# Two 64-row score products per head pair in two banks, and a two-pass first product of the compression, in a hybrid decoder block

## The chip, the cores and the metric

The kernel runs on one core of a Trainium2 chip. The metric is the device time of one execution in microseconds (us), as the median of several runs. Matrix products run on TensorE (PE in the rows, its weight loads PEld), elementwise work on VectorE (DVE) and ScalarE (ACT); GpSimd (POOL) and SyncE (SP) mainly issue transfers (DMA).

## The reference, cut to what matters

256 tokens of width 1024 go through one block. Two attention branches of 8 heads of 64 run side by side (with 256 tokens every block that a query may look at is selected, so branch A is causal attention and branch B is the gated sum of a compressed, a selected and a window part). A gated merge, an output projection and a mixture of 16384 one-neuron experts follow.

```python
# branch A, per head:  s = q k^T * scale ; causal mask ; softmax ; o = p v
s_own = jnp.einsum('hqd,hld->hql', qc, k_own)
# branch B, compressed keys and values, per group g:
blocks = t[:, idx] + pos_emb[None, None, :, None, :]
flat = blocks.transpose(0, 3, 1, 2, 4).reshape(B, G, n_cmp, CMP_LEN * D)
return jax.nn.gelu(flat @ w1 + b1) @ w2 + b2        # n_cmp = 15, CMP_LEN * D = 2048, w1: 2048 x 256
# branch B: o = g0 * o_cmp + g1 * o_slc + g2 * o_win, each a masked softmax over its keys
```

## The kernel before, in words

Float32 products whose result needs the accuracy are made from two rounded halves: a helper `split` (L104) lets ScalarE cast to a high half (`whi`, `hhi`, `bhi`) and VectorE subtract it to get a low half (`wlo`, `hlo`, `blo`). Each product is then three passes, high by high, high by low and low by high (`mm3`, L126). Weights come through `load_piece` (L109): a transfer of 512 KB into `wraw`, then a split, three buffers each.

**The order of the first stage.** PE runs the projections of the input (`token_proj`, `ps_proj`, L168 to L171), and among them the two calls of `compress` (L300): keys (kv = 0) after the second 512-wide projection, values (kv = 1) after the third. Then come four merge gates (`merge_gate` L378, products L121, L122 and L124 inside `cols_proj`, 24 products of 256 columns each). The queries and keys are normalised per head, rotated and transposed by `to_dt` (L256) into `qTA`, `qTB`, `kTA` and `kTB`, with the 64 dimensions of the two heads of a pair on the 128 partitions.

**The compression** (`compress`). The 30 blocks (2 groups of 15) have 2048 inputs each, 16 chunks of 128. Its first product `ph` (L129 to L131) has the 30 blocks as the stationary operand and 256 columns of `w1` as the moving one: 16 chunks by three passes, 48 products of 256 columns, in four weight pieces. Then `hrow` copies the result, two transposes `pht` (L323) turn it round, ScalarE applies the bias and the GELU (`hid`), and `po` (L330) is the second product.

**The attention** (`attn_unit`, L405). There are 24 units: for each half h of the 256 queries four pairs of heads of branch A, and four pairs by two kinds of branch B. With h = 0 a query sees 128 keys, with h = 1 it sees 256. A unit makes on PE a mask product (`ps_s`, L408, bfloat16, identity by mask, 256 columns), a score product (L410, float32), transposes of the probabilities (`ps_pt`, L427) and the output products (`ps_y`, `ps_yb`, L432, 64 columns of the array each). In between VectorE takes the maximum (L413), ScalarE two exponentials (L417), VectorE scales (L423), and ScalarE copies the transposes (L429). So that one score product gives both heads of a pair side by side, the keys are padded with zeros: `kTA` and `kTB` have the shape [128, 4, 2, 256], where slice j holds head j's keys in its own 64 partitions and zeros in the other 64. GpSimd writes the zeros at the start (L182, L183), and `to_dt` fills the keys with two half-height copies on ScalarE (L265). Before the first half of branch B ends, `ps_sc` (L449), `ps_pct` (L468) and `ps_yb` (L473) do the compressed part.

**PSUM.** In this stage eight banks are shared out as four tags of two: `s` (scores), `tp` (transposes), `y` (outputs) and `mg` (merge gates 4 to 15, and later the up and output projections). The instructions of one engine run in a fixed order, which a list scheduler sets when the program is built, from priorities, buffers and its own estimates; so it also puts products of gates 4 and 5 among the attention where it expects PE to wait.

Behind that come gates 4 to 15, the up projection (`ps_up`), the output projection (`ps_o`), the query projection of the experts (`ps_q`) and the two long expert stages (`ps_u` L588, `acc` L855).

## Time and profile before

| | us |
|---|---|
| median of 3 runs | 940.72 (939.09 to 942.44) |
| the profiled execution, its own time | 938.46 |
| its span | 936.7 |
| the stretch that the change touches, first product to last attention product | 0 to 159.4 |

The profile is read by stages: for each stretch the busy time of every engine, then, in the stretch that the change touches, the instructions in order of time. A row's start is exact to about 0.01 us; a PE row's own length contains the time until the result has left the array and overlaps the next row, so what a product costs PE is read from start to start. "[0.81 <-ACT hid]" at a row's end is idle time of the engine before it and what ended it.

### The profile page before, as it was taken

To read this page: it belongs to the slowest core of one execution; us is meant where nothing else is said; L and a number is where in the kernel's file an instruction comes from. 1 tells how busy PE (TensorE), PEld (TensorE's weight loads), DVE (VectorE), ACT (ScalarE), POOL (GpSimd) and SP (SyncE) were. 2 spreads that over 40 slices of the span, in tenths; PEclk is the share of its full clock that TensorE was granted. 3 is DMA by queue.
4 is the path that set the end of the run, shared out by engine and by line. 5 is a ranking of instruction groups with operands and counts; after the bars stand their busy time and mean duration, and the time that the engine had idled before them with its cause. 6 is when DMAs were issued, how large, how long until landed. Compare 5 with 4: busy or idle time off the path is not lost.

```text
span 936.7 us, 17034 instructions
## 1 busy us (share of the span) xinstructions
PE 900.6 (96%) x6433; PEld 842.9 (90%) x6433; DVE 614.3 (66%) x1663; ACT 309.6 (33%) x768; POOL 218.4 (23%) x213
## 2 busy tenths in 40 slices
PE   8999999999999999999999999999989989998987
PEld 6778867998899999999999999999988888988986
DVE  5886876577567689997778788644445544444444
ACT  6766776545541221326555455300000000000000
POOL 2000000000100223233232233333344333443330
PEclk9999999999999999999999999999999999999999
DMA  7665401556556999999999999999999999999994
GB/s 242 191 213 190 159 1 47 183 185 210 169 173 235 331 392 365 376 373 328 350 334 352 354 339 347 354 378 403 357 369 399 400 380 403 385 392 401 400 398 185
DMA packets 79570, 281.96 MB, mean 301 GB/s; under 512 B 10176, under 2 KB 10432, under 8 KB 79488
## 3 DMA queue, kind: packets, MB, share of 16 engines
q1 hardware_dynamic: 51088, 177.63, 52.6%
q0 software_dynamic: 28400, 103.25, 29.2%
q8 instruction: 51, 0.84, 0.3%
q14 instruction: 31, 0.25, 0.1%
HBM read 278.64 MB, written 1.05 MB: 299 GB/s over the span
## 4 chain that ended last, share of the span: by engine, by line
PE 56%; DMA 28%; issue 7%; POOL 3%; DVE 3%; ACT 2%; DVEq 0%; POOLq 0%; ACTq 0%; SPq 0%
PE ps_u L588 28%; DMA grow<-in_v_dram,gidx 21%; PE ps_g L819 4%; POOL grow L611 3%; DMA grow<-in_u_dram,gidx 3%; PE ps_q L121 2%; PE ps_mg L124 2%; PE ps_mg L121 2%; PE ps_q L124 2%; PE ps_q L122 2%; PE ps_mg L122 2%; PE ps_s L410 2%; PE ps_proj L171 1%; PE ps_pt L427 1%; DVE wlo L106 1%
## 5 line engine op out<-in xcount | busy, mean ns | idle before, releaser
L855 PE MATMUL acc<-ga,uvraw 128*128 128x160 f32 x2048 | 292.9, 302 | 21.3 <-DMA uvraw<-in_v_dram 19.5
L855 PEld LDWEIGHTS acc<-ga,uvraw 128*128 128x128 f32 x2048 | 279.9, 190 | 34.2 <-DMA uvraw<-in_v_dram 32.3
L588 PE MATMUL ps_u<-h2f,uvraw 128*128 128x160 f32 x2048 | 287.3, 299 | 0.0
L588 PEld LDWEIGHTS ps_u<-h2f,uvraw 128*128 128x128 f32 x2048 | 280.7, 190 | 0.1
L633 DVE SCALAR_TENSOR_TENSOR accG<-grow,gwt,accG 128x1024 f32<-128x1024 f32 x94 | 120.8, 1285 | 137.0 <-DMA grow<-in_v_dram,gidx 136.9
L611 POOL DMA_INDIRECT grow<-in_u_dram,gidx x96 | 102.1, 1063 | 302.2 <-DVE gdot L622 149.1
L611 POOL DMA_INDIRECT grow<-in_v_dram,gidx x96 | 106.0, 1104 | 166.0 <-DVE mark L857 150.0
L622 DVE CUSTOM_DVE_ANT_0 grow<-grow,h2d 128x1024 f32<-128x1024 f32 x96 | 116.7, 1218 | 34.6 <-DMA grow<-in_u_dram,gidx 34.5
L106 DVE TENSOR_TENSOR wlo<-wraw,whi 128x1024 fp32r<-128x1024 f32 (+1 forms) x80 | 95.5, 1196 | 37.1 <-ACT whi L105 37.0
L105 ACT CAST whi<-wraw 128x1024 fp32r<-128x1024 f32 (+1 forms) x80 | 82.0, 1029 | 65.5 <-PE ps_q L122 13.9
L868 ACT COPY accT<-acc 128x320 f32<-128x320 f32 x2 | 0.9, 426 | 270.9 <-PE acc L855 270.9
L592 ACT ACTIVATE ga<-ps_u 128x160 f32<-128x160 f32 (+32 forms) x124 | 33.5, 271 | 143.7 <-PE ps_u L588 143.4
L814 ACT ACTIVATE og<-o,gT 128x128 f16<-128x128 f16 x160 | 61.9, 568 | 15.9 <-PE ps_g L819 14.5
L819 PE MATMUL ps_g<-og,o 128*128 128x128 f16 x320 | 44.4, 294 | 0.0
L819 PEld LDWEIGHTS <-o 128*128 128x128 f16 x320 | 36.3, 116 | 1.5
L168 PE MATMUL ps_proj<-whi,hhi 128*128 128x512 f32 (+1 forms) x96 | 36.3, 381 | 1.3 <-ACT hhi L205 1.0
L489 POOL DMA_DIRECT2D gain<-in_g_dram x1 | 0.5, 533 | 151.2 <-DVE wlo L106 151.2
L169 PE MATMUL ps_proj<-whi,hlo 128*128 128x512 f32 (+1 forms) x96 | 35.7, 378 | 0.0
L121 PE MATMUL ps_mg<-hhi,whi 128*128 128x256 f32 x128 | 32.3, 288 | 0.0
L596 DVE TENSOR_TENSOR ga<-ga,au 128x160 f32<-128x160 f32 (+32 forms) x68 | 16.8, 247 | 23.4 <-ACT au L595 22.9
L122 PE MATMUL ps_mg<-hlo,whi 128*128 128x256 f32 x128 | 31.9, 285 | 0.0
L121 PE MATMUL ps_q<-h2hi,whi 128*128 128x256 f32 x128 | 31.7, 285 | 0.2 <-ACT h2hi L105 0.2
(256 smaller groups left out, 1126.0 us busy)
## 6 DMA issues: line engine op xcount, KB each, us to landing
uvraw<-in_uT_dram SPq DMA_DIRECT2D x128, 512.0 KB, 6.8
uvraw<-in_v_dram SPq DMA_DIRECT2D x128, 512.0 KB, 7.2
wraw<-in_wqkv_dram SPq DMA_DIRECT2D x20, 512.0 KB, 4.7
wraw<-in_wmg_dram SPq DMA_DIRECT2D x16, 512.0 KB, 3.6
wraw<-in_wq_dram SPq DMA_DIRECT2D x16, 512.0 KB, 4.3
wraw<-in_w1kv_dram SPq DMA_DIRECT2D x8, 512.0 KB, 4.0
wraw<-in_wup_dram SPq DMA_DIRECT2D x8, 512.0 KB, 3.6
wraw<-in_wout_dram SPq DMA_DIRECT2D x8, 512.0 KB, 4.5
```

The costliest lines, as they stand in the source:

```text
L105: nc.scalar.copy(hi, src)
L106: state["dve"] = nc.vector.tensor_sub(lo, src, hi)
L121: nc.tensor.matmul(ps, lh, rh, start=i == 0, stop=False)
L122: nc.tensor.matmul(ps, ll if lo_last else lh, rh if lo_last else rl, start=False, stop=False)
L124: nc.tensor.matmul(ps, lh if lo_last else ll, rl if lo_last else rh, start=False, stop=i == NC - 1)
L588: state["pe"] = nc.tensor.matmul(ps, raw[:, c * P:(c + 1) * P], h2f[:, c, NG:], start=c == 0, stop=c == NC - 1)
L611: nc.gpsimd.indirect_dma_start(out=dst, out_offset=None, in_=src, in_offset=bass.IndirectOffsetOnAxis(ap=gidx[:, j:j + 1], axis=0))
L622: nc.vector.tensor_tensor_reduce(out=g, in0=g, in1=h2d[k], scale=1.0, scalar=0.0, op0=ALU.mult, op1=ALU.add, accum_out=gdot[:, j:j + 1])
L633: nc.vector.scalar_tensor_tensor(accG[:, k], g, gwt[:, j:j + 1], accG[:, k], op0=ALU.mult, op1=ALU.add)
L814: nc.scalar.activation(og[0][:, :, k], o1[:, :, k], AF.Copy, scale=gT[:, t0 + k:t0 + k + 1])
L819: nc.tensor.matmul(ps[:, k, :], o2[:, :, k], og[i][:, :, k], start=i == 0, stop=i == 1, skip_group_check=True)
L855: nc.tensor.matmul(acc[c // 2][:, c % 2, 0:ND], raw[:, c * P:(c + 1) * P], ga_at(i), start=i == 0 and c % 2 == 0, stop=i == NKEY - 1, skip ...
```

## The change

- `attn_unit`: the score tile gets one bank per head (`bank2`, two banks, two buffers, tag `s2`). The mask product becomes two of 128 columns, and the score product becomes two products of 64 rows, one per head and bank, each with 128 (h = 0) or 256 (h = 1) columns.
- No zero padding: `kTB` is half as large, of `kTA` one slice is used, the four large fills on GpSimd go, and `to_dt` always makes one copy of full height.
- The tag `mg` is gone, since `s2` takes four banks: gates 4 to 15, `ps_sc`, `ps_up`, `ps_o` and a warming product now take one bank of an `s2` buffer.
- `compress`: the high and the low half of the blocks lie side by side as 60 stationary columns, so one pass of the high weights serves both; the low weights need a second pass with 30 columns. The two halves of the result are added by a product with two stacked identities (`twice`, fetched by two small transfers), in place of the transpose.

```diff
+    def bank2(name):
+        return psum[-1].tile([P, 2, 512], F32, name=name, tag="s2")
...
-        kTB = ap.tile([P, 4, 2, S], F32, name="kTB")
+        kTB = ap.tile([P, 4, S], F32, name="kTB")
...
-        for t in (kTA, kTB, kcT):
-            nc.gpsimd.memset(t[0:HD, :, 1], 0.0)
-            nc.gpsimd.memset(t[HD:P, :, 0], 0.0)
+        nc.gpsimd.memset(kcT[0:HD, :, 1], 0.0)
+        nc.gpsimd.memset(kcT[HD:P, :, 0], 0.0)
...
-            if len(dst.shape) == 3:
-                nc.scalar.copy(dst[:, :, h * P:(h + 1) * P], pt)
-            else:
-                for j in range(2):
-                    r = slice(j * HD, (j + 1) * HD)
-                    nc.scalar.copy(dst[r, :, j, h * P:(h + 1) * P], pt[r])
+            nc.scalar.copy(dst[:, :, h * P:(h + 1) * P], pt)
...
+        twice = ap.tile([P, 2 * N_CMP], F32, name="twice")
+        for i in range(2):
+            r = slice(2 * N_CMP * i, 2 * N_CMP * (i + 1))
+            nc.gpsimd.dma_start(twice[r], consts[r, r])
...
-            bhi = sp.tile([P, 16, 2 * N_CMP], F32R, name="bhi")
-            blo = sp.tile([P, 16, 2 * N_CMP], F32R, name="blo")
-            split(bhi, blo, blk.rearrange("p c g n -> p c (g n)"))
-            ph = bank("ph", "s")[0:2 * N_CMP, 0:256]
-            pairs = []
+            nb = 2 * N_CMP
+            bhl = sp.tile([P, 16, 2 * nb], F32R, name="bhl")
+            split(bhl[:, :, 0:nb], bhl[:, :, nb:], blk.rearrange("p c g n -> p c (g n)"))
+            ph = bank("ph", "s")[0:2 * nb, 0:256]
             for i in range(4):
                 hi, lo = load_piece(w1kv[kv][:, i * DM:(i + 1) * DM])
-                pairs += [((bhi[:, 4 * i + k], blo[:, 4 * i + k]),
-                           (hi[:, k * 256:(k + 1) * 256], lo[:, k * 256:(k + 1) * 256])) for k in range(4)]
-            mm3(ph, pairs)
+                for k in range(4):
+                    r, last = slice(k * 256, (k + 1) * 256), i == 3 and k == 3
+                    if last:
+                        nc.tensor.matmul(ph[0:nb], bhl[:, 4 * i + k, 0:nb], lo[:, r], start=False, stop=False)
+                    nc.tensor.matmul(ph, bhl[:, 4 * i + k], hi[:, r], start=i + k == 0, stop=last)
+                    if not last:
+                        nc.tensor.matmul(ph[0:nb], bhl[:, 4 * i + k, 0:nb], lo[:, r], start=False, stop=False)
...
-                nc.tensor.transpose(pht[:, hc, 0:2 * N_CMP], hrow[0:2 * N_CMP, hc], C("ident")[0:2 * N_CMP, 0:2 * N_CMP])
+                nc.tensor.matmul(pht[:, hc, 0:nb], hrow[0:2 * nb, hc], twice[0:2 * nb], start=True, stop=True,
+                                 skip_group_check=True)
...
-            ps = bank("ps_mg", tag)[:, :S]
+            ps = (bank("ps_mg", tag) if tag else bank2("ps_mg")[:, 0])[:, :S]
...
-            s = bank("ps_s", "s").rearrange("p (j k) -> p j k", j=2)
-            nc.tensor.matmul(s[:, :, nk - P:nk], identb, maskb, start=True, stop=False,
-                             skip_group_check=True)
-            nc.tensor.matmul(s[:, :, 0:nk], qT[:, pair, h * P:(h + 1) * P], kf[:, :, 0:nk],
-                             start=False, stop=True, skip_group_check=True)
+            s = bank2("ps_s")
+            for j in range(2):
+                nc.tensor.matmul(s[:, j, nk - P:nk], identb, maskb[:, 0], start=True, stop=False,
+                                 skip_group_check=True)
+            for j in range(2):
+                r = slice(j * HD, (j + 1) * HD)
+                nc.tensor.matmul(s[:, j, 0:nk], qT[r, pair, h * P:(h + 1) * P], kf[r, 0:nk],
+                                 start=False, stop=True, skip_group_check=True)
```

The scheduler sets the order of PE anew. At the start of the attention (`ps_s` scores, `ps_mg` gate products, `ps_pt` transposes of the probabilities) PE had this order before the third unit, where these are the last two of seven gate products:

```order
L122 MATMUL ps_mg_1811<-hlo_85,whi_1814 128x256
L121 MATMUL ps_mg_1811<-hhi_84,whi_1814 128x256
L408 LDWEIGHTS identb_1201
L408 MATMUL ps_s_1244<-maskb_1203,identb_1201 128x2x128
L410 MATMUL ps_s_1244<-kTA_87,qTA_86 128x2x128
L427 MATMUL ps_pt_1218<-cst_58,pr_1211 128x128 x2
```

and with the change:

```order
L418 MATMUL ps_s_1188<-kTA_87,qTA_86 128x128 x2
L414 LDWEIGHTS identb_1162
L414 MATMUL ps_s_1209<-maskb_1164,identb_1162 128x128
L414 LDWEIGHTS identb_1162
L414 MATMUL ps_s_1209<-maskb_1164,identb_1162 128x128
L418 MATMUL ps_s_1209<-kTA_87,qTA_86 128x128 x2
L435 MATMUL ps_pt_1181<-cst_58,pr_1174 128x128 x2
```

The gate products between the second and the third unit are gone from there; the first of them stands behind the last score of the stage now, and the mask and score products have doubled.

In the first units of the second half (h = 1, branch A; `ps_yb` are outputs of branch B) PE had before:

```order
L408 LDWEIGHTS identb_1201
L408 MATMUL ps_s_1485<-maskb_1203,identb_1201 128x2x128
L410 MATMUL ps_s_1485<-kTA_87,qTA_86 128x512
L432 MATMUL ps_yb_1313<-pT_1438,vB_91 64x128 x2
L427 MATMUL ps_pt_1455<-cst_58,pr_1447 128x128 x2
```

and with the change:

```order
L414 LDWEIGHTS identb_1162
L414 MATMUL ps_s_1470<-maskb_1164,identb_1162 128x128
L414 LDWEIGHTS identb_1162
L414 MATMUL ps_s_1470<-maskb_1164,identb_1162 128x128
L418 MATMUL ps_s_1470<-kTA_87,qTA_86 128x256
L440 MATMUL ps_yb_1282<-pT_1419,vB_91 64x128 x2
L435 MATMUL ps_pt_1438<-cst_58,pr_1430 128x128
L418 MATMUL ps_s_1470<-kTA_87,qTA_86 128x256
L435 MATMUL ps_pt_1438<-cst_58,pr_1430 128x128
```

The two score products of this unit no longer stand side by side: outputs and a transpose of other units lie between them.

## Rows read from the trace of the kernel before

**Rows 1.** The page: the chain that ended last, share of the span by engine.
```profile
PE 56%; DMA 28%; issue 7%; POOL 3%; DVE 3%; ACT 2%; DVEq 0%; POOLq 0%; ACTq 0%; SPq 0%
```
**Rows 2.** Busy time by stage: the attention's two halves; stretch, length, engines, PE clock, DMA.
```profile
106.80:126.60 19.80, 18.47 (x141) 12.83 (x139) 14.81 (x58) 15.40 (x62) 0.00 (x0) 1.00 0.14 50
126.60:159.40 32.80, 32.80 (x250) 20.57 (x247) 23.64 (x75) 23.71 (x74) 0.53 (x1) 1.00 0.01 2
```
**Rows 3.** The chain of waits: one score of each half, and eight full-size products.
```profile
116.04 0.43 PE ps_s L410 x2
...
130.25 0.86 PE ps_s L410 x2
...
267.44 0.89 PE ps_s L668 x8
```
**Rows 4.** The start: GpSimd in order of time, DMA between 4 and 5 us, two issues.
```profile
2.01 0.98 POOL L182 MEMSET kTA<- 64x1024 f32 x1
...
6.21 0.57 POOL L208 DMA_DIRECT2D cst<-in_consts_dram  x1
...
4.00:5.00 1.00, 1.00 (x4) 0.59 (x3) 0.00 (x0) 0.00 (x0) 0.94 (x1) 1.00 1.05 365
...
sml<-in_small_dram POOLq DMA_DIRECT2D x1, 538.0 KB, 5.7
...
cst<-in_consts_dram POOLq DMA_DIRECT2D x1, 432.0 KB, 4.4
```
**Rows 5.** PE in order of time: the key compression's waits, and the one behind it.
```profile
45.45 0.30 PE L130 MATMUL ph<-wlo,bhi 128*30 128x256 f32 x1 [1.28 <-DVE wlo L106]
...
47.78 0.30 PE L130 MATMUL ph<-wlo,bhi 128*30 128x256 f32 x1 [0.76 <-DVE wlo L106]
...
52.92 0.24 PE L323 MATMUL pht<-cst,hrow 30*128 30x30 f32 x1 [0.81 <-ACT hid L325]
```
**Rows 6.** The value compression: its first product, the next projection's, a cast before.
```profile
63.78 0.28 PE L129 MATMUL ph<-whi,bhi 128*30 128x256 f32 x1
...
69.33 0.40 PE L168 MATMUL ps_proj<-whi,hhi 128*128 128x512 f32 x1
...
66.44 1.23 DVE L106 TENSOR_TENSOR wlo<-wraw,whi 128x1024 fp32r<-128x1024 f32 x1 [0.58 <-ACT whi L105]
```
**Rows 7.** PE in order of time: a product of 30 rows between full-size ones.
```profile
69.80 0.39 PE L168 MATMUL ps_proj<-whi,hhi 128*128 128x512 f32 x1
70.11 0.24 PE L323 MATMUL pht<-cst,hrow 30*128 30x30 f32 x1
70.29 0.66 PE L259 MATMUL pt_dt<-cst,q_h 128*128 128x128 f32 x4
```
**Rows 8.** PE in order of time: output products that write alternating halves of the partitions.
```profile
119.34 1.09 PE L473 MATMUL ps_yb<-pcT,vc 15*64 15x128 f32 x16
120.36 0.33 PE L427 MATMUL ps_pt<-cst,pr 128*128 128x128 f32 x1
```
**Rows 9.** PE in order of time: eight 16-bit products of 128 columns.
```profile
437.34 1.10 PE L819 MATMUL ps_g<-og,o 128*128 128x128 f16 x8
438.26 3.03 PE L588 MATMUL ps_u<-h2f,uvraw 128*128 128x160 f32 x21
```
**Rows 10.** The attention's start: ScalarE and PE in order of time.
```profile
107.57 1.77 ACT L265 COPY kTB<-pt_dt 64x512 f32<-64x512 f32 x3
109.35 0.37 ACT L417 ACTIVATE pr<-ps_s,nm 128x128 f32<-128x128 f32 x1
...
110.21 0.27 PE L408 MATMUL ps_s<-maskb,identb 128*128 128x256 bf16 x1 [1.33 <-ACT pr L417]
```
**Rows 11.** Groups by line, 106.8 to 159.4: gate products among the attention (count, busy, mean).
```profile
L121 PE MATMUL ps_mg<-hhi,whi 128*128 128x256 f32 x13 | 3.9, 323 | 0.0
L122 PE MATMUL ps_mg<-hlo,whi 128*128 128x256 f32 x13 | 3.7, 301 | 0.0
...
L124 PE MATMUL ps_mg<-hhi,wlo 128*128 128x256 f32 x8 | 2.2, 354 | 0.0
```

More of the change, by code (lines that the diff above doesn't have):

```diff
@@ L366, in block_kernel @@
         compress(1)
-        qk_post(ps_ka, kTA, gq("gk", 0), 1.0)
+        qk_post(ps_ka, kTA[:, :, 0], gq("gk", 0), 1.0)
         ps_qb = token_proj(wqkv[3], 512)
@@ L441, in block_kernel @@
             for pair in range(4):
-                attn_unit(qTA, pair, h, kTA[:, pair],
+                attn_unit(qTA, pair, h, kTA[:, pair, 0],
                           lambda j, kb: vA[:, kb, (2 * pair + j) * HD:(2 * pair + j + 1) * HD],
@@ L445, in block_kernel @@
             y_out(0, h, yb)
-            sc = bank("ps_sc", "s")[:, :128].rearrange("p (h n) -> p h n", n=16)
+            sc = bank2("ps_sc")[:, 0, :128].rearrange("p (h n) -> p h n", n=16)
             for pair in range(4):
@@ L483, in block_kernel @@
         for i in range(4, 16):
-            merge_gate(i, "mg")
+            merge_gate(i, None)
         spx.close()
@@ L492, in block_kernel @@
         for c_out in range(NC):
-            ps = bank("ps_up", "mg").rearrange("p (b t) -> p b t", b=2)
+            ps = bank2("ps_up")[:, 0].rearrange("p (b t) -> p b t", b=2)
             hi, lo = load_piece(wup[c_out])
@@ L516, in block_kernel @@
             for h in range(NH):
-                ps = bank("ps_o", "mg")
+                ps = bank2("ps_o")[:, 0]
                 mm3(ps, [((mhi[:, c, h * P:(h + 1) * P], mlo[:, c, h * P:(h + 1) * P]),
@@ L547, in block_kernel @@
                                             xn[sum(SETS[:k]):sum(SETS[:k + 1]), 0].rearrange("p a b -> p (a b)"))
-                ph = bank("ps_heat", "s")[:, 0:2 * P]
+                ph = bank2("ps_heat")[:, 0, 0:2 * P]
                 for i in range(HEAT):
```

2 lines of the change are left out of this document (1 added, 1 removed).

## The prediction

> **What bounds the kernel now.** I read the chain that ended last first. It lies 56% on TensorE (PE) and 28% on transfers [rows 1]. The transfers belong to the expert stages, which this change leaves alone and which start when the stages ahead of them are done; so what is saved or lost before them arrives at the end in full. The change touches the first 159.4 us. Next I read the busy time by stage: in the attention's second half PE is busy for 32.80 of 32.80 us, while ScalarE has 23.71 and VectorE 23.64; in the first half PE has 18.47 of 19.80 [rows 2]. The clock is at full speed, 1.00, the 2.4 GHz level, in both. So the attention is bound by PE, strictly in its second half and with some waits in its first, and the last view is PE in order of time.
>
> **What a score costs.** A unit's score product takes 0.43 us with 256 columns and 0.86 with 512, in two passes on the array that the profile shows as two records [rows 3]. Half of the array's work there is with zeros.
>
> **The sum, part by part.** It is made against the profiled execution's own time, 938.46 us, which is 2.26 below the median of 940.72. A measurement of this kernel can tell about 0.3% from no change, 2.8 us.
>
> *1. The start.* Four fills of about 0.95 us leave GpSimd, behind which two loads of constants were issued, the first at 6.21 us [rows 4]. They are issued some 3.8 us earlier now. Their 970 KB (432 and 538) then share the transfer engines with the input rows and the first weights, and these engines are full there (share 1.05, 365 GB/s) [rows 4]. At worst all of the constants go first: 970 KB / 365 GB/s = 2.7 us later. At best the last projection weight, which shared with them before, comes a little sooner: -0.7. The bytes needed by about 13 us are the same, so I take +0.3. The two small loads of `twice` stand behind these on GpSimd's queue, which then has nothing until the attention's end: nothing.
>
> *2. The compression.* Each call goes from 48 products to 32, one per 0.116 us: (69.33 - 63.78) / 48 [rows 6]. That is 16 x 0.116 = 1.86 us on PE each. For the values PE does not wait in that stretch, so the question is what is late next: the fourth weight piece's cast, whose buffer comes free with the first piece. Its low half starts at 66.44 and lasts 1.23 [rows 6]; the first piece frees its buffer four products, 0.46 us, sooner, so that half is ready at 67.2, and seven products, 0.81, remain: 68.0 in place of 69.33, which is -1.3. For the keys PE waits for VectorE's low halves, 1.28 and 0.76 us, and 0.81 for ScalarE behind it [rows 5]. After the second wait seven products remain in place of eleven, -0.46; the scheduler puts two projection products of 0.235 ((69.80 - 69.33) / 2, [rows 6, 7]) ahead of it, -0.47; and it moves more projection work ahead of the third wait, so I count about 0.5 of that. Together -1.4, between -0.5 (only the four products) and -2.2. The new `pht` has a second record in each of four products, about 0.05 each: +0.2. The compression gives **-2.5**.
>
> *3. The attention.*
> - **Overlap.** No row here has two products that use different rows of the array. The nearest have different columns: sixteen records of 128 columns, alternating between the two halves of the output, take 120.36 - 119.34 = 1.02 us, 0.064 each [rows 8], where eight full-size records of 128 columns take 0.89, or 0.111 each [rows 3]. Two at a time, then, and a little for entering and leaving. If rows behave as columns do, a pair costs 0.215 less with h = 0 and 0.43 less with h = 1. But the scheduler has set the two products of a pair side by side in 17 of the 24 units only (11 with h = 0, 6 with h = 1); in the others a full-size or half-column product lies between, and nothing overlaps. 11 x 0.215 + 6 x 0.43 = **-4.9**. At the other end, no overlap: 0.
> - **Changes of the array's shape.** A 30-row product between full-size ones starts 0.08 us after the slot before it ends (69.80 + 0.235 = 70.03 to 70.11), and with its own pass holds the next one up by 0.18 [rows 7]: some 0.1 for each change. The sixteen records say the same: 1.02 - 8 x 0.107 = 0.16 (0.107 is half of a 256-column record) for entering and leaving. Counted along PE's order in both programs, the attention goes from 50 such changes to 92, because scores were full-size before and are half-row now. 42 x 0.11 = **+4.6**, between +1.3 (0.03 each, where the next weights are already there) and +5.0.
> - **Masks.** One mask of 256 columns becomes two of 128 with a weight load each. Eight 16-bit products of 128 columns take 438.26 - 437.34 = 0.92, 0.115 each, not half of a 256-column one [rows 9]; so the pair costs between nothing more (the load hidden) and 0.12 more, 0 to 2.9 in 24 units. I take the middle, **+1.4**, since the first load can hide behind the full-size product ahead of it.
> - **Gate products.** Before, 13 + 13 + 8 = 34 of them stood among the attention [rows 11]; with gates and scores in the same banks 19 do, all near the end. 15 x 0.12 (256 columns, as in the compression) = **+1.8** moves behind the attention, where PE has no waits to hide it. Their weights were cast long before, and nothing else queues behind them.
> - **The first wait.** PE stands until 110.21 for exponentials that start at 109.35, behind half-height copies of the keys, three of them 1.77 us [rows 10]. Two of four copies go, 2 x 0.59: **-1.2**.
> - **Other waits.** With fewer gate products as filling and a shorter chain from score to maximum I take 0, between -1 and +3 (0.12 in each of 24 units).
>
> The attention sums to -4.9 + 4.6 + 1.4 + 1.8 - 1.2 = **+1.7**. Up and output projections keep two buffers each; the keys of branch A are copied well before use: nothing.
>
> All together: 0.3 - 2.5 + 1.7 = -0.5, so 937.9 against the profile's 938.46, and **940.2** against the median.
>
> **Rule and row.** On the shape the rows show 0.08 us into a half-row product and about as much out of it [rows 7]. The Trainium skill, "TensorEngine Tiling (Array Packing)", Key Properties, says that a change of tiling mode, not only of tile, drains TensorE; by it every one of the 42 new changes costs. The Trainium skill, "TensorE: Matmul & The Clock Gate", Measured speedup vs the span model, counts a pack of small products as one product and some 4 ns per further tile; by that alone the changes would cost nothing and the sum would be 4.6 lower, an estimate. The trace agrees with the first of the two.
>
> **The rivals.**
> - *It gains.* The new changes of shape are cheap, as a half-row score goes straight on to half-column outputs that had to drain anyway; at 0.03 each they cost 1.3 in place of 4.6, and the second mask load hides: -0.5 - 3.3 - 1.4 = -5.2, 935.5. For it: in the first half PE has waits in which a change could hide [rows 2]. Against: rows 7, where the neighbours were ready.
> - *It loses: the two halves don't overlap.* Different rows with all columns write the same partitions of two banks, which no row of this trace shows. Then the 4.9 is missing while the changes are still paid: +4.4, 945.1. It decides for slower as soon as less than about a third of the overlap is there (4.9 x 0.67 = 3.3, which with -0.5 is 2.8). For it: nothing direct; against: columns overlap fully [rows 8].
> - *It loses another way: the attention becomes bound by its chain.* Without gate products to fill in and with the gates behind the scores, every unit waits for its softmax: +3 in waits, 943.2. Against: ScalarE and VectorE are busy for 72% in the second half.
> - *The change does not do what it says:* if the scheduler parts more pairs than counted, or fewer, it is 0.43 per unit; that is inside the range.
>
> **How the numbers follow.** I give the forecast (within 2.8 us of no change) 0.50, the gain 0.28, no overlap 0.13, the chain 0.09. Faster by over 0.3% is 0.28, within it 0.50, slower 0.22. The forecast's own terms reach from about 937.5 to 943; the range takes in the gain and most of the second loss: 935.2 to 944.5.
>
> **What would show it.** In the profile after: value compression from its first product to the next projection in about 4.2 us in place of 5.55; two score records in one place at the same time and a pair of h = 1 in about 0.43 us plus 0.1 on each side; the first exponential about 1.2 us sooner; 19 gate products among the attention; the stretch from the first mask to the last output about 52.5 us, as before (52.6). I am wrong if half-row records stand one after another, if the gaps at changes of shape are well under 0.05 us, or if the start before 17 us moves by over 1 us.

## The result and the profile after

The changed kernel is slower: 950.52 us median (947.08 to 952.38, 7 runs) beside 942.44 for the kernel before on the same chip (939.09 to 945.92, 7 runs). The ratio is 1.0075, with a 95% interval of 1.0047 to 1.0104, so 7.1 us lost (4.4 to 9.8). The prediction was 940.2 with a range to 944.5: wrong, and on the wrong side. The profiled execution of the kernel after spans 946.4 us, that of the kernel before 936.7. In some executions of kernels with the new attention (five of twelve of e1, four of nine of e7, two of twelve of e9) the mean clock was lower (0.969 to 0.988) and the time up to 978 us: the ratios below leave these out, but not those of e10 and e11, whose executions all had a mean clock under 0.985.

The busy time by stage of the kernel after answers [rows 2] and shows the first thing that I had not reckoned with. Columns: stretch and length, then busy us (and instructions) of PE, PEld, VectorE, ScalarE and GpSimd, the granted clock, the DMA share and GB/s.

```profile
10.30:17.10 6.80, 6.74 (x27) 5.79 (x25) 5.67 (x17) 5.85 (x17) 0.00 (x0) 0.50 0.47 146
17.10:43.30 26.20, 26.18 (x131) 22.06 (x131) 18.98 (x34) 19.30 (x27) 0.00 (x0) 1.00 0.63 200
43.30:51.20 7.90, 4.47 (x33) 3.58 (x32) 7.16 (x13) 4.48 (x6) 0.00 (x0) 1.00 0.67 205
51.20:54.60 3.40, 3.40 (x12) 2.39 (x11) 2.81 (x6) 2.39 (x3) 0.00 (x0) 0.50 0.79 258
...
110.51:130.20 19.69, 18.37 (x166) 12.57 (x163) 15.11 (x61) 15.00 (x62) 0.00 (x0) 1.00 0.15 50
130.20:164.84 34.64, 34.35 (x281) 22.66 (x280) 21.53 (x70) 23.14 (x72) 0.55 (x1) 1.00 0.01 2
```

Twice TensorE runs at 0.50, its 1.2 GHz level: from 10.3 to 17.1 us, and from 51.2 to 54.6. The kernel before had 1.00 in this whole stretch of its profiled execution. One execution could be luck, but the mean clock over all of them says the same: 0.989 to 0.994 in the seven of the kernel after (median 0.991), against a median of 0.997 in the 101 of the kernel before that ran beside the experiments. An estimate from these two medians, 0.006 of 945 us, is that the lower clock cost at most 5.7 us, if TensorE was busy whenever it was low; no run separates this from the waits that go with it. The second half of the attention is 34.64 us in place of 32.80.

The next rows, in order of time, show the start (they answer [rows 4]; the columns are start, duration, engine, line, operation, and in brackets the idle time ahead and what ended it).

```profile
2.25 0.57 POOL L210 DMA_DIRECT2D cst<-in_consts_dram  x1
...
7.30 0.66 ACT L108 CAST whi<-wraw 128x560 fp32r<-128x560 f32 x1 [1.21 <-DMA wraw<-in_wkv_dram]
...
8.02 0.40 PE L171 MATMUL ps_proj<-whi,hhi 128*128 128x280 f32 x1 [1.47 <-ACT whi L108]
...
8.26 0.29 DVE L408 CAST maskb<-cst 128x256 bf16<-128x256 f32 x1 [5.33 <-DMA cst<-in_consts_dram]
8.46 0.35 DVE L208 SCALAR_TENSOR_TENSOR hlo<-pt_row,sml,hhi 128x128 fp32r<-128x128 f32 x1
...
8.86 0.39 PE L172 MATMUL ps_proj<-whi,hlo 128*128 128x280 f32 x1 [0.45 <-DVE hlo L208]
```

The constants are issued 4 us earlier, as predicted. But the first weights are cast at 7.30 (5.99 before), and VectorE has the mask's cast at the head of its queue: it waits for the constants until 8.26, and the first low half of the input behind it starts at 8.46 (6.13 before). TensorE stands for 1.47 and 0.45 us, and then its clock falls. In the kernel before the mask was cast at 15.43 us, behind the low halves.

In the key compression ([rows 5]) these rows matter:

```profile
47.16 0.31 PE L322 MATMUL ph<-wlo,bhl 128*30 128x256 f32 x1 [1.66 <-DVE wlo L109]
...
47.63 1.22 DVE L109 TENSOR_TENSOR wlo<-wraw,whi 128x1024 fp32r<-128x1024 f32 x1
...
48.00 0.28 PE L320 MATMUL ph<-whi,bhl 128*60 128x256 f32 x1
48.95 1.04 ACT L108 CAST whi<-wraw 128x1024 fp32r<-128x1024 f32 x1 [1.71 <-DVE wlo L109]
50.05 0.50 PE L171 MATMUL ps_proj<-whi,hhi 128*128 128x512 f32 x1 [1.77 <-ACT whi L108]
50.39 0.40 PE L172 MATMUL ps_proj<-whi,hlo 128*128 128x512 f32 x1
50.62 0.28 PE L322 MATMUL ph<-wlo,bhl 128*30 128x256 f32 x1
```

The last low half that the compression needs is ready at 47.63 + 1.22 = 48.85. But TensorE's next instruction is a projection product whose own weights are only cast from 48.95 on. It starts at 50.05, and the compression goes on at 50.62: 1.77 us lost to two products that I had booked as a gain. The value compression ([rows 6]) takes 72.56 - 66.66 = 5.9 us in place of 5.55, up to the next projection. TensorE waits twice near its end, and a third time behind its last product, for the projection's weights:

```profile
66.66 0.28 PE L320 MATMUL ph<-whi,bhl 128*60 128x256 f32 x1
66.88 1.26 ACT L375 ACTIVATE vA<-ps_proj,rs 128x512 f32<-128x512 f32 x2
68.78 1.05 ACT L108 CAST whi<-wraw 128x1024 fp32r<-128x1024 f32 x1 [0.64 <-DVE rope L254]
...
69.88 0.33 PE L320 MATMUL ph<-whi,bhl 128*60 128x256 f32 x1 [0.25 <-ACT whi L108]
71.14 0.30 PE L322 MATMUL ph<-wlo,bhl 128*30 128x256 f32 x1 [0.93 <-DVE wlo L109]
71.47 1.05 ACT L108 CAST whi<-wraw 128x1024 fp32r<-128x1024 f32 x1 [1.63 <-DMA wraw<-in_wqkv_dram]
...
72.56 0.50 PE L171 MATMUL ps_proj<-whi,hhi 128*128 128x512 f32 x1 [0.42 <-ACT whi L108]
```

In the attention ([rows 3]), a pair of half-row scores with h = 0, a unit with h = 1 whose halves stand apart, and one whose halves stand together (x2 is one half, x4 a pair):

```profile
117.03 0.49 PE L418 MATMUL ps_s<-kTB,qTB 64*128 64x128 f32 x4
117.45 0.44 PE L440 MATMUL ps_y<-pT,vA 128*64 128x128 f32 x4
...
129.49 0.28 PE L414 MATMUL ps_s<-maskb,identb 128*128 128x128 bf16 x2
129.70 0.70 PE L418 MATMUL ps_s<-kTA,qTA 64*128 64x256 f32 x2
130.32 0.44 PE L440 MATMUL ps_yb<-pT,vB 128*64 128x128 f32 x4
130.69 0.33 PE L435 MATMUL ps_pt<-cst,pr 128*128 128x128 f32 x1
130.95 0.70 PE L418 MATMUL ps_s<-kTA,qTA 64*128 64x256 f32 x2
...
141.48 0.70 PE L418 MATMUL ps_s<-kTB,qTB 64*128 64x256 f32 x4
142.11 0.67 PE L440 MATMUL ps_y<-pT,vA 128*64 128x128 f32 x8
```

From start to next start, a pair takes 142.11 - 141.48 = 0.63 us and one half alone 130.32 - 129.70 = 0.62. The halves do overlap fully, and a half alone costs as much as both. With h = 0 a pair takes 0.42. The two masks of a unit take 129.70 - 129.49 = 0.21, one of 256 columns took 0.11.

### The profile page after: what moved, and what is told of

Read it like the earlier page. It is cut to its first block, busy times and chain, and to the rows that moved or that the text cites. A ratio compares the mean times of both kernels' runs of the same rounds, so it can differ in the third digit from the quotient of the medians.

```text
span 946.4 us, 17119 instructions
## 1 busy us (share of the span) xinstructions
PE 906.3 (96%) x6477; PEld 848.0 (90%) x6477; DVE 613.5 (65%) x1663; ACT 308.3 (33%) x764; POOL 216.8 (23%) x211
## 4 chain that ended last, share of the span: by engine, by line
PE 56%; DMA 27%; issue 8%; DVE 4%; POOL 3%; ACT 2%; DVEq 0%; POOLq 0%; ACTq 0%; SPq 0%
PE ps_u L596 27%; DMA grow<-in_v_dram,gidx 21%; PE ps_g L827 4%; POOL grow L619 3%; DMA grow<-in_u_dram,gidx 3%; PE ps_q L124 2%; PE ps_mg L127 2%; PE ps_mg L124 2%; PE ps_q L127 2%; PE ps_mg L125 2%; PE ps_q L125 2%; DMA wraw<-in_wqkv_dram 2%; PE ps_s L418 1%; PE ps_pt L435 1%; PE ps_proj L171 1%
## 5 line engine op out<-in xcount | busy, mean ns | idle before, releaser
L863 PE MATMUL acc<-ga,uvraw 128*128 128x160 f32 x2048 | 293.3, 302 | 23.4 <-DMA uvraw<-in_v_dram 21.3
L619 POOL DMA_INDIRECT grow<-in_u_dram,gidx x96 | 104.0, 1083 | 300.9 <-DVE gdot L630 151.0
L171 PE MATMUL ps_proj<-whi,hhi 128*128 128x512 f32 (+1 forms) x96 | 38.9, 408 | 3.7 <-ACT whi L108 3.7
L172 PE MATMUL ps_proj<-whi,hlo 128*128 128x512 f32 (+1 forms) x96 | 37.7, 399 | 0.4 <-DVE hlo L208 0.4
```

The lines of the kernel that those rows point to most:

```text
L171: nc.tensor.matmul(ps(h), lh, hi[:, r], start=c == 0, stop=False)
L619: nc.gpsimd.indirect_dma_start(out=dst, out_offset=None, in_=src, in_offset=bass.IndirectOffsetOnAxis(ap=gidx[:, j:j + 1], axis=0))
L863: nc.tensor.matmul(acc[c // 2][:, c % 2, 0:ND], raw[:, c * P:(c + 1) * P], ga_at(i), start=i == 0 and c % 2 == 0, stop=i == NKEY - 1, skip ...
```

## The experiments

All thirteen ran beside the kernel before on the same chips. Their profiled executions are cut at the same places (us): "first 512" is the start of the first projection product of 512 columns; "key compr." runs from the first to the last start of a product `ph`, "value compr." from the first `ph` to the next projection; "to gates" is the time from the first 512 to the first merge gate, "behind" the time from the attention's end to the up projection.

| kernel | first 512 | key compr. | value compr. | to gates | attention | behind | ratio, 95% interval |
|---|---|---|---|---|---|---|---|
| before | 17.2 | 7.9 | 5.5 | 77.2 | 52.7 | 30.5 | 1 |
| after | 19.9 | 8.0 | 5.9 | 78.1 | 54.4 | 32.3 | 1.0075 [1.0047, 1.0104] |
| e1 | 18.5 | 9.0 | 6.1 | 78.3 | - | 32.3 | 1.0071 [1.0032, 1.0110] |
| e2 | 21.3 | 7.4 | 5.5 | 77.5 | 52.7 | 30.5 | 1.0030 [1.0002, 1.0057] |
| e3 | 17.3 | 9.8 | 5.9 | 79.7 | 52.7 | 30.5 | 1.0001 [0.9968, 1.0035] |
| e4 | 18.2 | 9.7 | 5.8 | 80.5 | 54.4 | 32.3 | 1.0088 [1.0058, 1.0118] |
| e5 | 18.3 | 7.1 | 5.6 | 76.0 | 52.7 | 30.5 | 1.0018 [0.9994, 1.0041] |
| e6 | 18.2 | 8.7 | 8.9 | 81.0 | 52.7 | 30.5 | 1.0067 [1.0045, 1.0089] |
| e7 | 17.0 | 7.8 | 5.5 | 76.9 | 54.4 | 32.3 | 1.0058 [1.0032, 1.0084] |
| e8 | 18.3 | 8.7 | 8.9 | 80.9 | 52.7 | 30.5 | 1.0058 [1.0031, 1.0085] |
| e9 | 18.6 | 7.7 | 6.1 | 78.4 | 54.4 | 32.3 | 1.0040 [1.0002, 1.0077] |
| e10 | 18.4 | 6.6 | 5.7 | 76.6 | 74.0 | 32.4 | 1.0226 [1.0182, 1.0271] |
| e11 | 17.5 | 6.3 | 5.4 | 76.8 | 72.5 | 32.4 | 1.0239 [1.0185, 1.0292] |
| e12 | 18.7 | 7.6 | 5.9 | 81.9 | 52.6 | 30.5 | 1.0038 [1.0010, 1.0066] |
| e13 | 18.3 | 8.4 | 5.6 | 79.2 | 52.6 | 30.5 | 1.0015 [0.9988, 1.0043] |

A ratio here is good to about 0.3%, so the stages often tell more than the totals. But each kernel's stages come from one execution, and the first 512 alone differs by up to 1.7 us between kernels that start alike. The attention of e1 is left out: in its profiled execution the clock was 0.50 for 47.8 us from 113.4 us on.

### The start: e1, e2, e4

e1, on the changed kernel:

```diff
+        for r in (slice(0, HD), slice(HD, P)) * 2:
+            nc.gpsimd.memset(kTA[r, :, 1], 0.0)
         nc.gpsimd.memset(kcT[0:HD, :, 1], 0.0)
```

> The changed kernel with four fills of the old size put back on GpSimd ahead of the loads of constants (they fill the unused half of kTA), so that these loads are issued as late as before. Theory (the loads, issued 4 us earlier, delay the first weights and VectorE behind the mask's cast, TensorE stands, and its clock falls between 10 and 17 us): the first product of the first 512-column projection is at 17.2 us again in place of 19.9, the granted clock is 1.00 between 10 and 17 us, and the span goes from 946.4 to about 943.6. Rival (the start is lost for another reason, or its loss is made good later): the span stays at 946. In the key compression the theory has the clock fall again after the waits there, with or without the fills.

e2 moves the two loads of constants (L208, L209) ahead of the fills in the kernel before.

> The kernel before with one thing moved: the two loads of constants are issued ahead of the fills, as early as in the changed kernel. Theory: the start loses the same 2.8 us as in the changed kernel (17.15 to 19.9), with a clock below 1.00 between 10 and 17 us, and the span goes from 936.7 to 939.5. Rival (the early loads are harmless; what is late in the changed kernel comes from its other parts): 936.7.

e4, on the changed kernel (`hl` is the last low half of the input rows):

```diff
-        nc.vector.tensor_copy(maskb, C("mask").unsqueeze(1).to_broadcast([P, 2, P]))
+        with tc.issue_after(hl.ins):
+            nc.vector.tensor_copy(maskb, C("mask").unsqueeze(1).to_broadcast([P, 2, P]))
```

> The changed kernel with the loads as early as it has them, but the cast of the mask on VectorE put behind the last low half of the input rows, so that VectorE does not wait for the constants ahead of the first of them. If VectorE behind the mask's cast is what makes the start late, the first 512-column projection product is back near 17.2 to 17.8 us and the span near 943.6. If the late first weights (cast at 7.30 in place of 5.99) are enough by themselves, it stays at 19 to 20 us and the span at 946.

e2 agrees with the theory: 2.8 us lost (0.2 to 5.4), the clock at 0.51, and every stage behind the start within 0.5 us of before. The picture in the trace is not quite that of the kernel after: here the first weights are cast at 9.39, later still, and it is for them that TensorE waits.

```profile
9.39 0.66 ACT L105 CAST whi<-wraw 128x560 fp32r<-128x560 f32 x1 [3.30 <-DMA wraw<-in_wkv_dram]
...
10.11 0.60 PE L168 MATMUL ps_proj<-whi,hhi 128*128 128x280 f32 x1 [3.56 <-ACT whi L105]
```
```profile
10.10:17.00 6.90, 6.05 (x23) 5.32 (x24) 4.94 (x16) 4.71 (x15) 0.00 (x0) 0.51 0.25 85
```

e1 is half a confirmation: no fall of the clock ahead of 17 us and the first 512-column product at 18.5 in place of 19.9, but not at 17.2, and its total can't be told from the changed kernel's. Put together, the eleven kernels with late loads on GpSimd have that product between 17.0 and 18.7, 18.1 on average; the profile of before, with 17.2, was an early one. The three with early loads have 18.2 (e4), 19.9 and 21.3. So the early loads cost 2.5 us by the two stages that have the mask's cast ahead as well (19.9 and 21.3), 1.7 with e4 counted in, and 2.8 (0.2 to 5.4) by e2's ratio. The clock fell ahead of 17 us in all three, but also, from 8.0 to 8.9 us on, in four of the eleven (e8, e9, e10, e12): the early loads are not its only cause. e4 divides the suspects: with the mask's cast out of the way the product comes 1.8 us sooner, but the clock still fell, from 10.0 to 13.4 us, and again in the key compression; the total did not gain. How the loss is shared between the cast and the late weights stays open.

### The compression: e3, e5, e6, e8

e3 is the kernel before with the new compression alone.

> The kernel before with the two-pass compression alone. My prediction had -2.5 for it: span 934.2, value compression 4.2 us in place of 5.55. The theory now: after the key compression's waits the clock falls as in the changed kernel (0.50 for some 2 us), which takes back about 2 us there, and the value compression is held up by a late low half: span 936 to 937. Rival (the changed kernel's second fall of the clock came from the late start alone): no fall, 934.2.

It shows no gain: 1.0001, and 79.7 us from the first 512-column product to the gates in place of 77.2. The clock fell from 45.2 to 52.0, after TensorE was busy for 2.47 of 4.20 us:

```profile
41.00:45.20 4.20, 2.47 (x19) 1.77 (x17) 4.17 (x10) 2.80 (x5) 0.00 (x0) 1.00 0.63 191
45.20:52.00 6.80, 5.33 (x20) 4.13 (x21) 4.73 (x10) 3.44 (x4) 0.00 (x0) 0.50 0.69 224
```

The ratio and the single execution do not say the same here: the stretch is 2.5 us longer, and the total by 0.1 (-3.0 to +3.3). There are two suspects, the order and the clock. e5 takes the projection products out of the key compression (the first diff), e6 fills TensorE's gaps (the second), and e8 does both:

```diff
-                    nc.tensor.matmul(ph, bhl[:, 4 * i + k], hi[:, r], start=i + k == 0, stop=last)
+                    state["ph"] = nc.tensor.matmul(ph, bhl[:, 4 * i + k], hi[:, r], start=i + k == 0, stop=last)
...
-        ps_va = token_proj(wqkv[2], 512)
+        with tc.issue_after(state["ph"].ins):
+            ps_va = token_proj(wqkv[2], 512)
```
```diff
                     if not last:
+                        nc.tensor.matmul(ph, heat[:, 0:2 * nb], heat[:, 0:256], start=False, stop=False)
```

> The kernel before with the two-pass compression, and the projection that follows the key compression held behind its last product on TensorE (no projection products between the last pieces). Theory A (two projection products that the scheduler sets ahead of the last low-half products wait for weights of their own, 0.79 us, and hold the compression up): key compression from first to last product 9.75 us before this edit, 8.3 or less after it. Theory B (the lower clock alone makes it long; TensorE stands the same time for VectorE's low halves): still 9 to 10 us, with a clock of 0.50 for 3 to 7 us there. Span 938 to 940 by A, 942 to 943 by B.

> The kernel before with the two-pass compression, and behind 30 of its 32 whole products one more product with zeros into the same output (it adds nothing), so that TensorE has as much to do there as before the change. Theory (the clock falls because the two passes leave TensorE idle between the low halves): no fall of the clock in the key compression, first to last product 7.9 to 8.5 us in place of 9.75, and with the projection products still in their place a wait of 0.8 us for their weights; span 938 to 939. Rival (the clock falls for another reason): it falls as before, 9.7 us or more, and the span is 945 because the added products cost 3.5 us.

> Both edits of e5 and e6 on the two-pass compression alone. If the wait for the projection's weights and the clock are both at work, this one is the shortest of the three: key compression 7.9 us or less, the start of the merge gates no later than the kernel before has it (94.3), span 936 to 938. If VectorE's low halves set the end there whatever TensorE does, it is about the kernel before, not the -2.5 of the prediction.

e5 agrees with theory A: 7.1 us. But the clock held too, in a profiled execution that was the fastest of e5's twelve (span 933.8 us), so e5 alone cannot tell A from a clock that stayed up by chance. The table divides the two, with one execution for each kernel. With the scheduler's order the key compression took 8.0 us where the clock fell only at its end (after) and 9.0 to 9.8 where it fell earlier (e1, e3, e4); with the order mended it took 6.3 to 7.6 at the full clock (e5, e10, e11, e12) and 7.7 where the clock fell late (e9). So both suspects are at work.

```profile
46.21 0.31 PE L326 MATMUL ph<-wlo,bhl 128*30 128x256 f32 x1 [1.70 <-DVE wlo L106]
...
47.94 0.30 PE L326 MATMUL ph<-wlo,bhl 128*30 128x256 f32 x1 [0.62 <-DVE wlo L106]
```
```profile
41.56:48.77 7.21, 4.29 (x33) 3.37 (x32) 6.88 (x15) 4.50 (x6) 0.00 (x0) 1.00 0.65 203
```

What is left there are waits for VectorE, which is busy for 6.88 of 7.21 us. TensorE, with 4.29, no longer matters, so of the 1.86 us that the two passes save on it 0.8 arrive. In all, e5's stretch to the gates is 76.0 us, 1.2 less than before; by the ratio (1.0018) there is no gain, neither on the kernel before nor on e3 (1.0001). So what the mended order is worth is shown by the stages alone.

e6 and e8 missed. The clock did hold (1.00 through both compressions), which speaks for the theory of the clock, but the filling was far too dear: TensorE was busy for all of 8.8 us in either compression. One of these zero products (`heat`, 16-bit) in the middle of a group adds 0.34 us (66.12 - 65.54 = 0.58 for three products against 0.233 for two), where the expectation reckoned with 3.5 us for 30 of them, 0.12 each.

```profile
65.54 0.28 PE L324 MATMUL ph<-whi,bhl 128*60 128x256 f32 x1
65.75 0.29 PE L326 MATMUL ph<-heat 128*60 128x256 bf16 x1
65.98 0.30 PE L327 MATMUL ph<-wlo,bhl 128*30 128x256 f32 x1
66.12 0.28 PE L324 MATMUL ph<-whi,bhl 128*60 128x256 f32 x1
```

### The compression's bound: e12, e13

```diff
-    def head_norm(h, ps, nh, gains, qscale):
+    def head_norm(h, ps, nh, gains, qscale, eng=nc.vector):
...
-                nc.vector.tensor_mul(q[:, g0:g0 + n], q[:, g0:g0 + n], gain.unsqueeze(1).to_broadcast([P, n, HD]))
+                eng.tensor_mul(q[:, g0:g0 + n], q[:, g0:g0 + n], gain.unsqueeze(1).to_broadcast([P, n, HD]))
```

The four rotations go with it; `eng` is GpSimd for the first queries and the keys of branch A.

> e5 (the kernel before with the ordered two-pass compression) and the gain and rotation of the first queries' and keys' head norms on GpSimd in place of VectorE (1.8 us of VectorE for each of four halves). Theory (VectorE's low halves set the time of the compression): waits of TensorE for low halves fall from 2 to 3 us to under 1, key compression 4.5 to 6 us in place of 7.1, value compression 4.2 to 4.8 in place of 5.4, start of the merge gates 2 to 4 us sooner than the kernel before (94.3); span 933 to 935. Rival (something else sets it: ScalarE's high halves or the landing of the weights): key and value compression as in e5, and no gain.

> The kernel before with the same norms on GpSimd and its own three-pass compression. Theory: the waits for low halves (2.0 us) go here too, key compression 5.9 to 6.5 in place of 7.9, value compression 5.55 as before since TensorE bounds it; merge gates 1.5 to 2.5 us sooner; e12 is 1 to 3 us better than this. Rival: GpSimd's slower norms make the transposes of the queries wait, and it is slower than the kernel before.

Neither theory held, and both kernels are slower to the gates (81.9 and 79.2 us). The moved products take 1.74 us on GpSimd in place of 0.68, and VectorE's small instructions beside them grow: the two `kcd` take 764 ns each, 272 before (the rows are e13's).

```profile
L348 DVE TENSOR_TENSOR kcd<-kc,sml 15x128 f32<-15x128 f32 x2 | 1.5, 764 | 0.0
```
```profile
L245 POOL TENSOR_TENSOR q_h<-q_h,sml 128x512 f32<-128x512 f32 x4 | 7.0, 1738 | 37.4 <-DVE q_h L243 37.4
```

The Trainium skill, "SBUF — State Buffer", section "SBUF: two separate sides", says that VectorE instructions with two inputs in SBUF and GpSimd instructions that read there hold a shared pair of ports in turn, the other one blocked for the whole instruction; the rows agree. So VectorE was not relieved, and the two runs don't settle the question that they were for: that VectorE bounds the key compression rests on the rows of e5 above and of the kernel before below.

### The attention: e7, e9, e10, e11

e7 is the changed kernel with e1's fills and the old three-pass compression, so that the attention is all that is new.

> The changed kernel with the old three-pass compression and with four fills on GpSimd ahead of the loads, so that the attention with half-row scores is all that is new. Theory: the attention takes 54.4 us from the first mask to its end in place of 52.7, the gates behind it 32.3 in place of 30.5, span 936.7 + 3.5 = 940.2; nothing before the attention moves by more than 1 us. Rival (the attention's part of the loss came from the late start): 52.7 and 30.5, span 936.7. In one look of e1 the clock was 0.50 from 113 to 161 us: if half-row scores are what lets it fall, some executions here are 10 to 25 us longer with a mean clock under 0.985, and none of the kernels with the old attention are.

```profile
106.40:126.50 20.10, 18.78 (x170) 12.76 (x167) 15.25 (x61) 15.40 (x65) 0.00 (x0) 1.00 0.14 49
126.50:160.72 34.22, 33.94 (x280) 22.47 (x276) 21.38 (x69) 22.68 (x70) 0.54 (x1) 1.00 0.01 1
```

The theory holds: 54.4 and 32.3 us, +1.7 and +1.8, nothing ahead of it moves (the gates start 0.4 us sooner), and the ratio gives 5.5 us (3.0 to 7.9). So the attention's loss of 3.5 us is its own; the 2 us more of the ratio are within its interval and in no stage here. The expectation's last sentence came true as well: four of the nine executions took 966 to 970 us at a mean clock of 0.970 to 0.975. Of 180 executions of kernels with the old attention (101 of the kernel before, 79 of e2, e3, e5, e6, e8, e12 and e13) one had a mean clock under 0.985 (the kernel before, 0.655 and 1280 us). What sets the fall off in one execution and not in the next stays open.

e9 has e1's and e5's edits on the changed kernel.

> The changed kernel with two repairs: the fills back on GpSimd (constants' loads as late as before), and the projection held behind the key compression as in e5. What is left is the new attention and a two-pass compression that does not wait for a projection's weights. Theory (the parts add up: attention +3.5, early loads +2 to +3, the wait in the compression +1 to +2): start of the attention no later than in the kernel before (106.8) give or take 1 us, attention 54.3, gates 32.3, so the span about 936.7 + 3.5 - 0.6 = 939.6; ratio 1.002 to 1.005. Rival (there is a part of the loss that these three do not hold): the start of the attention stays 2.5 us late and the span at 943 to 946.

The ratio, 1.0040 (1.0002 to 1.0077), is within the theory's; the profiled execution is not, with the attention 2.6 us late, as the rival had it: the clock fell in it from 8.0 to 14.8 us and from 49.0 to 52.4, though the first projection product was on time (6.4 us). So the late loads and the mended order do not keep the clock up by themselves, and the interval is too wide to tell theory from rival.

e10 sets TensorE's order in the attention by hand, on e9: scores of a unit, outputs of the second unit before, transposes of the one before.

```diff
+        def step(g):
+            with tc.issue_after(pe[0].ins):
+                next(g, None)
...
-                attn_unit(qTA, pair, h, kTA[:, pair, 0],
+                unit(qTA, pair, h, kTA[:, pair, 0],
```

(`attn_unit` becomes a generator that stops ahead of its transposes and its outputs; `pe[0]` is the last matmul issued.)

> e9 with TensorE's order in the attention set by hand: the two half-row scores of each of the 24 units stand side by side, and the outputs of two units before follow them. In the changed kernel 14 halves stand alone, and one alone took 0.63 us (256 columns) or 0.42 (128), as long as a pair. Theory (a lone half costs a pair's time): seven pairs saved, 6 x 0.63 + 0.42 = 4.2 us less in the attention, 50.1 in place of 54.3. Rival (the new order makes TensorE wait for the exponentials, since no unit can run ahead any more): 53 or more, with waits in the first half where a unit is short.

e11 is e10 without the fills, with the constants loaded on the weights' queue.

> e10 without the fills, and the two loads of constants on the weights' own queue behind the first four weight pieces in place of GpSimd's queue. Theory (the start is lost because the constants' 970 KB go ahead of the first weights): first projection product at 6.5 us or sooner, first 512-column product at 17 us, no fall of the clock before 17 us; span as e10 or up to 1 us less. Rival (the loads' place does not matter, the start varies from execution to execution anyway): first projection product anywhere between 6.4 and 8, as in the other runs.

All 24 pairs stand together in e10, and pairs with h = 1 at the full clock take 0.63 us where TensorE does not wait (151.47 - 150.84 below); so the price of a pair is confirmed. But the rival holds for the time:

```profile
107.50:111.00 3.50, 1.99 (x18) 1.32 (x16) 2.38 (x7) 2.89 (x11) 0.00 (x0) 1.00 0.75 259
111.00:148.50 37.50, 33.96 (x184) 21.70 (x182) 16.98 (x65) 16.35 (x63) 0.00 (x0) 0.50 0.01 4
```
```profile
111.00 0.80 PE L421 MATMUL ps_s<-kTA,qTA 64*128 64x128 f32 x4
111.73 0.69 PE L445 MATMUL ps_y<-pT,vA 128*64 128x128 f32 x4
...
150.84 0.70 PE L421 MATMUL ps_s<-kTA,qTA 64*128 64x256 f32 x4
151.47 0.67 PE L445 MATMUL ps_y<-pT,vA 128*64 128x128 f32 x8
```

The fixed order makes TensorE wait in the first units (1.99 us busy of 3.50), the clock falls at 111.0, and it comes back only at 148.5. All six executions of e10 and of e11 had a mean clock of 0.969 to 0.982. That the waits bring the fall on is not shown: in e1, without the fixed order, the clock fell as well. What kept pairs save in all stays open, since neither profiled execution had them at the full clock throughout. e11's start was on time (6.7 and 17.5 us) with no fall of the clock ahead of the attention; one execution can't tell that from the luck of the others.

No version beat the kernel before. e3, e5 and e13 (1.0001, 1.0018, 1.0015) are level with it.

## Why the prediction was wrong

The step that failed is the one from TensorE's work to time. The sum booked what two passes save on TensorE in the compression as 2.5 us won, put the earlier loads at next to nothing and had no term for the clock; and in the attention it booked a wait that only moved. By the stages the parts are: start +2.5, compression +1.9, attention +1.7 and gates behind it +1.8, together 7.9 beside the measured 7.1 (4.4 to 9.8). The forecast for the same terms was +0.3, -2.5, and +1.7 for the last two together. The ratios of the kernels with one part each divide it otherwise, e2 +2.8, e3 +0.1 and e7 +5.5, each good to some 3 us. So that start and attention lose is shown. The compression's +1.9 rests on single executions: e3's interval (-3.0 to +3.3 us) holds it and, just, the forecast's -2.5 as well, while e5's (-0.6 to +3.9) does not hold the -2.5.

**The start (+0.3, measured +2.5).** "The bytes needed by about 13 us are the same" was true and beside the point. I priced the transfers and looked at GpSimd's queue, but not at what the earlier loads let the scheduler do on VectorE: it put the mask's cast ahead of the first low half, so VectorE's queue waited for the last bytes of the constants, and the first weights were late as well; how much each cost is open (e4). The forecast's own bound for all of the constants going first, 2.7, was nearer. And I had no term for the clock. The prediction named "if the start before 17 us moves by over 1 us" as a sign of its failure, and it did, by 2.8 in the trace.

**The compression (-2.5, measured +1.9).** The +1.9 is the mean of the four kernels with the two passes in the scheduler's order (after, e1, e3, e4: 78.1, 78.3, 79.7, 80.5 to the gates, 79.1) less that of the three with the old compression in its place (before, e2, e7: 77.2). Four steps failed.
- The keys' "-0.46" for four products fewer behind the second wait took TensorE's share as the measure. In the kernel before VectorE was already busy for 7.97 of 8.00 us there (TensorE 5.96), so work taken from TensorE could bring little.

```profile
41.10:49.10 8.00, 5.96 (x50) 4.86 (x48) 7.97 (x15) 4.81 (x7) 0.00 (x0) 1.00 0.69 200
```

- "The scheduler puts two projection products ahead of it, -0.47": I took their duration as filling without asking whether their own weights were there. They waited 1.77 us, with the compression queued behind them. In the four kernels in which they stand behind it (e5, e9, e10, e11) the stretch is 76.0, 78.4, 76.6 and 76.8, 76.9 on average, 2.2 less.
- "For the values PE does not wait, -1.3": the stretch became 0.4 longer. I moved only the buffer's release forward; the last weights' cast came no sooner, since ScalarE had two copies of `vA` and a wait ahead of it (66.88 and 68.78 in the rows above), and the low half behind it had to wait in turn. So the products took 71.87 - 66.66 = 5.21 us from first to last start, only 0.2 less than before, and the 0.42 behind them is the wait for the next projection's weights, whose cast could only start at 71.47 (the row above). With a third of TensorE's work gone, the pace of the casts is what is left.
- Idle time on an engine that no longer bounds was taken as free. Here it was followed by a fall of the clock in the key compression, each time behind waits of TensorE, in all four kernels with two passes in the scheduler's order (after, e1, e3, e4) and in one of five with the order mended (e9; not e5, e10, e11, e12). With three passes (before, e2, e7, e13) and with the zero products (e6, e8) it did not fall there.

**The attention (+1.7 with its gates, measured +3.5).** The price of a pair was right, and the sum over the stretch was not. Right were the full overlap of row halves (0.63 for a pair, as the 0.43 + 0.2 of the forecast), 0.1 us at each change of shape, the 19 gate products, 1.8 us of gates behind, and the first exponential 1.3 us sooner (1.25 us behind the first mask in place of 2.54). By the Trainium skill, "TensorEngine Tiling (Array Packing)", Key Properties, a change of tiling mode drains TensorE; the 0.2 us around a lone half agree. The forecast for the stretch itself was -0.1 (52.5 us, with the gates' +1.8 behind it); it became +1.7. Adding up the times from one start on TensorE to the next by kind of product, waits included (before, after):

| product | before | after | difference |
|---|---|---|---|
| masks | 2.67 | 4.95 | +2.28 |
| scores | 16.76 | 18.86 | +2.10 |
| transposes | 9.05 | 10.14 | +1.09 |
| outputs (ps_y, ps_yb) | 13.35 | 13.81 | +0.46 |
| compressed branch (ps_sc, ps_pct) | 3.46 | 3.75 | +0.29 |
| gates | 7.34 | 2.82 | -4.52 |

- "Masks: I take the middle, +1.4" was +2.28: 48 masks of 128 columns take 0.103 us each, 24 of 256 took 0.111. The upper bound, 2.9, was nearer.
- Overlap and changes, -4.9 + 4.6, came out on scores, transposes, outputs and the compressed branch at +3.9, TensorE's waits among them included. A pair with h = 1 saves 0.95 - 0.63 = 0.32, but a unit whose halves stand apart pays 2 x 0.63 - 0.95 = 0.31 more, and six of twelve do; so the h = 1 units together gain nothing at all.
- The gates fell by 4.52 where fifteen products are worth 1.8. Of the other 2.7, 1.33 is the wait at 110.21 [rows 10], which stood behind a gate product; the rest is that gate products stood in more places among products of another kind before, where one took 0.20 to 0.61 in place of 0.12. But TensorE's idle time in the stretch, 1.33 us before, is 1.61 after, 1.32 of it behind scores. "Other waits: 0" and "first wait -1.2" treated as saved what had only changed its place.

One reading was a little off, without weight in the sum: the eight full-size records of [rows 3] take 0.81 us from start to next start, 0.101 each; 0.89 is a length.

**The rivals.** "The two halves don't overlap" fell. "It loses another way: bound by its chain, +3" was near in size but not the mechanism: VectorE and ScalarE are no busier than before (21.53 and 23.14 of 34.64 us), and TensorE's idle time rose by 0.28 us only. None of the rivals was a loss ahead of the attention, where by the stages half of it lies, and by the ratios a third.

## What to carry to other kernels

Work taken from an engine is worth what the next one to be late allows: before booking the gain, lay its wait against the producer's busy share in the same stretch, as VectorE's 7.97 of 8.00 us before the change. When the scheduler moves an instruction forward, ask when its own inputs land, and what is queued behind it on that engine: a mask's cast and two projection products, each moved ahead by some places, cost, by the stages, more than the whole compression was to save. And a narrow product pays its changes of shape per run of such products, not per product, so count runs in the order that is really issued.

## What I had not expected of the hardware

- TensorE's clock fell to 1.2 GHz after short waits, none of them longer than 1.8 us in the kernel after: after 1.47 and 0.45 us at the start, after 1.66 and 1.77 in the key compression. The same kernel before, with waits of 1.28 and 0.76 us there, kept 2.4 GHz in its profiled execution.
- Once down in the attention with half-row scores, it stayed down while TensorE was busy for 33.96 of 37.50 us (e10), and a pair that takes 0.42 us at the full clock took 0.73 (111.73 - 111.00).
- A 16-bit product of zeros with 256 columns, put between products of the wider type of one group, added 0.34 us, where a mask of the same size ahead of full-size scores takes 0.11.
